# Scale and bias of two norms moved behind the products that read them

## The chip, the cores and the metric

The kernel runs on one core of a Trainium2 chip. A core has five engines with queues of their own: TensorE (PE, with its weight loads as PEld), VectorE (DVE), ScalarE (ACT), GpSimd (POOL) and SyncE (SP), which here issues all DMAs in order. The metric is the device time of one execution in microseconds. Lower is better.

## The reference

One layer of a hybrid diffusion block over 512 latent tokens and 256 context tokens of width 1024, in fp32. What matters for the change, cut down:

```python
# spatial gating, in the token mixer: 8 groups of 128 channels, chunks of 128 tokens
u, v = split(gelu(z_sgu), 2, axis=-1)
v = layer_norm(v, sgu_ln_g, sgu_ln_b)                # over 1024 channels
v = einsum('gpq,bnqgc->bnpgc', sgu_w, v) + sgu_b     # mixes the tokens of a chunk
y_s = u * v

# second sub-layer: norm, modulation, 16 experts that each choose 64 tokens
h = layer_norm(x1) * (1 + sc2) + sh2
aff = softmax(h @ router_w);  gate, idx = top_k(aff.T, 64)
ye = (silu(h[idx] @ exp_w1) * (h[idx] @ exp_w3)) @ exp_w2 * gate
x2 = layer_norm(ALPHA * x1 + gt2 * segment_sum(ye, idx))

# low-rank inputs of the RWKV branch: decay and rate of both directions
w0 + tanh(dw) @ w2          # dw has 64 columns for each direction
a0 + da @ a2
```

`sc2`, `sh2` and their like come from a projection of the conditioning vector (`ada_w`).

## The kernel before, in words

Scratch tiles of 4 KB a partition come from two pools: `T(...)` takes one of 32 slots of the pool `big`, `K(...)` one of 17 of the pool `keep`. A tile's slot goes to a later tile when its last reader is done, and the later tile's first writer waits for that. SyncE, TensorE and ScalarE work in program order all through; VectorE and GpSimd do so inside `manual_schedule()` blocks, and elsewhere a planner orders them by its costs.

Stages in order of time: first norms and modulation; the RWKV columns, eight blocks of 128 channels (L575 on); the gate stage, a list `UNITS` of 32 units with hooks between them (L1035 on); the scan over 12 chunks in both directions by a written plan (`PLAN`, L1062); readout, branch and out projections, the first and second norm and the router; the top-k; and 16 experts, whose weights (`we`, 1 MB a load, a ring of 16 double slots that lies over the pool `big`) are loaded by SyncE as slots come free.

- Token-mixer products split each fp32 operand into a rounded high half H (ScalarE) and the rest L (L160, VectorE or GpSimd), and TensorE adds H·H, H·L and L·H. `zw` streams the weights; `fill` steps it until three split weights wait, so a unit's `fill` makes the weights of the unit two later.
- `pair_x` (L295) takes the columns `dw` and `da` (128 partitions, the two directions in the halves, 256 context then 512 latent tokens). For each direction it makes a tile with the high half in both partition halves (ScalarE copy, DMA to the other half) and one with the rest beside zeros (GpSimd memset, VectorE subtraction): eight tiles in all. `prep_a` multiplies them with `w2` and `a2`.
- In the gate stage's first unit come the spatial norm's statistics and, for each of four tiles `vg`, three VectorE passes (L1031 to L1033): normalise, times `sgu_ln_g`, plus `sgu_ln_b`, the latter two as rows held in all partitions. Then `u_z(g)` projects group g, and `u_s(g)`, two units later, multiplies `vg` with `swt` and adds `sgu_b`.
- The modulation's later rows are summed on VectorE by `ada_part`, one of eight pieces behind each unit's weights. When the eighth is issued, `ada_row` follows in the same unit: two matmuls with `ones` (`adr`), two ScalarE copies, a store to `Mo`.
- `out_ln` makes the second norm `h2` with ScalarE (L146) and then two GpSimd passes over 128x1024 (L1269, L1270) with the rows `sc2` and `sh2`. The router does not read `h2`: it multiplies `x` with router weights that `router_cols` has scaled, out of `R["s2c"]`, which holds `sh2` and 1 + `sc2` by columns.
- `gather` (L1450) multiplies four `h2` tiles with one-hot matrices of two experts' chosen tokens; the result `xe` has channels on partitions and is copied from PSUM by ScalarE, four blocks of 128 channels at a time (one or two for the first pair).

Of the kernel before, what the change touches and what calls it, by code (L numbers as in the profile page):

```python
# [7 lines left out]
F32 = mybir.dt.float32  # L8
# [19 lines left out]
LN_EPS = 1e-5  # L28
GN_EPS = 64e-5
DEC = float(__import__("math").exp(-0.5))  # L30
NKEEP = 17
NBIG = 32

PC = {}
_n = 0
for _k, _w in (("w0", 16), ("a0", 16), ("k_k", 8), ("k_a", 8), ("lnx_g", 8), ("lnx_b", 8), ("r_k", 8),
               ("shift", 81), ("ada_b", 16), ("ln1_g", 8), ("ln1_b", 8)):
    PC[_k] = _n
    _n += _w
NPC = _n  # L40
# [3 lines left out]
def block_kernel(es: ExitStack, tc, x, ctx, cT, ada_w, ada_b, pc, rows, w_ch, w_vs, w2, a2, g2, sgu_w,  # L44
# [247 lines left out]
            V.tensor_tensor(w[h], t[h], w[h].bitcast(F32), OP.subtract)  # L292

    def pair_x(t):
        hs = []  # L295
        for d in range(2):
            h, o = slice(64 * d, 64 * d + 64), slice(64 - 64 * d, 128 - 64 * d)
            x2 = T([128, TT], "xp", F32R)
            S.activation(x2[h], t[h], AF.Copy)
            SY.dma_start(x2[o].bitcast(F32), x2[h].bitcast(F32))  # L300
            lo = T([128, TT], "xl", F32R)
            G.memset(lo[o].bitcast(F32), 0.0)
            V.tensor_tensor(lo[h], t[h], x2[h].bitcast(F32), OP.subtract)
            hs.append((x2, lo))
        return hs

    for k in range(KT):
# [101 lines left out]
    def prep_a(ct, d):  # L409
        s = st_[ct]  # L410
        cs = slice(ct * 128, ct * 128 + 128)
        p2 = P("b2")
        ev = s["ev", d] = []
        for o, lst, src, bias, off in (("g", w2p, dwt, "w0", TC), ("a", a2p, dat, "a0", 0)):
            p = P("b1")
            w, (xh, xl) = lst[d][:, cs], src[d]
            for o_, t_ in ((p, slice(TC, TT)), (p2[:, off:off + TC], slice(0, TC))):
                mm(o_, w, xh[:, t_], True, False)
                mm(o_, w, xl[:, t_], False, True)
            ev.append((o, p, p2[:, off:off + TC], col(bias, d * 8 + ct)))  # L420

    def prep_tanh(ct, d):
# [141 lines left out]
    def ada_part(k, w):  # L564
        wi, k = divmod(k, 8)
        a = late["a", wi]
        V.scalar_tensor_tensor(a, w, sC[:, k:k + 1], a, op0=OP.mult, op1=OP.add)
        if k == 4 and wi < 3:
            ada_begin(wi + 1)
        if k == 7:  # L570
            late["row"].append(a)

    zw.pre = -1
    with tc.manual_schedule():
# [183 lines left out]
    def statics(_):  # L758
        for d in range(2):
            st_tp["zn", d] = K([128, 2, KT, C], "zn")  # L760
            G.memset(st_tp["zn", d], 0.0)
        st_tp["o1"] = K([128, 2, 2, KT, 32], "o1")
        S.activation(st_tp["o1"].rearrange("p a b c i -> p (a b c i)"), zcol.to_broadcast([128, D]), AF.Copy)

    def statics_ro():
# [12 lines left out]
    Md = dp.tile([KT, 128, TL], F32, name="Md")  # L778
    Gd = dp.tile([KT, 128, TL], F32, name="Gd")
    def ada_row(wi):  # L780
        a = late["row"].pop(0)
        m = T([128, D], "mod")
        for h in range(2):
            hs = slice(h * 512, h * 512 + 512)
            p = P("adr")
            mm(p, ones, a[:, hs])
            S.activation(m[:, hs], p, AF.Identity, bias=1.0 if wi == 2 else 0.0)
        spills.append((Mo[wi], m))
# [131 lines left out]
                else:  # L920
                    V.tensor_tensor(dst, dst, p[hs], OP.add)

    sg_g, sg_b, sb_r = row(0), row(1), row(2)
    swt = T([128, 8, 128], "swt")
    SY.dma_start(swt, sgu_w)
    ug, gg_, late_mul = {}, {}, []
    ysH, ysL = [], []
    def u_z(g):
        pl, _ = zmm(zw.get(zi["u", g]), False)
# [3 lines left out]
    def u_s(g):  # L933
        p = P("sgu")
        for i in range(4):
            mm(p[:, i * 128:i * 128 + 128], vg[i][:, g * 128:g * 128 + 128], swt[:, g, :])
        t = T([128, 4, 128], "sgt")
        V.tensor_tensor(t, p.rearrange("p (a b) -> p a b", a=4),
                        sb_r[:, None, g * 128:g * 128 + 128].to_broadcast([128, 4, 128]), OP.add)
        u = ug.pop(g)  # L940
        V.tensor_mul(u, t.rearrange("p a b -> p (a b)"), u)
        if g % 2 == 0:
            ysH.append(K([128, 2, TL], "ysH", F32R))
            ysL.append(K([128, 2, TL], "ysL", F32R))
        H, L = ysH[g // 2][:, g % 2, :], ysL[g // 2][:, g % 2, :]
        S.activation(H, u, AF.Copy)
        V.tensor_tensor(L, u, H.bitcast(F32), OP.subtract)
# [68 lines left out]
    def hook(*key):  # L1016
        for f, a in HOOK.get(key, ()):
            f(a)
# [5 lines left out]
    with tc.manual_schedule():  # L1024
        hook("u", -1)
        mv4 = cp.tile([128, 4, 2], F32, name="mv4")
        for i in range(4):
            ln_stats(vg[i], mv4[:, i, :])
        r4 = rstd(mv4[:, :, 1], 4, LN_EPS)
        for i in range(4):  # L1030
            V.tensor_scalar(vg[i], vg[i], mv4[:, i, 0:1], r4[:, i:i + 1], op0=OP.subtract, op1=OP.mult)  # L1031
            V.tensor_mul(vg[i], vg[i], sg_g)
            V.tensor_add(vg[i], vg[i], sg_b)  # L1033
        lag = []
        for t, j in UNITS:  # L1035
            zw.eng = V
            run[t](j)
            if t == "u":
                lag.append(j)
            if lag and (len(lag) > 2 or t != "u"):  # L1040
                u_s(lag.pop(0))
            if t == "s" and j == 0:
                while lag:
                    u_s(lag.pop(0))
            hook(t, j)
            while len(late_mul) > (t == "b"):
                mul(*late_mul.pop(0))
            if t in "sa":
                flush()
            if late["row"]:  # L1050
                ada_row(late["wi"])
                late["wi"] += 1
        hook("end", 0)

    flush()
# [180 lines left out]
    def out_ln(half, outs, ps):  # L1236
        tiles = [HALF[half][o] for o in outs]
        n = len(tiles)
        mv = sm.tile([128, n, 2], F32, name=nm("mv"), tag=f"mv{n}")
        for q, (o, i) in enumerate(zip(outs, tiles)):  # L1240
            t = acc[i] = K([128, D], "x1")
            st = sm.tile([128, 2, 6], F32, name=nm("st"), tag="st")
            for h, hs in enumerate(HS):
                V.tensor_mul(t[:, hs], ps[o, h], R["gt1"][:, hs])
                V.scalar_tensor_tensor(t[:, hs], R["x", i][:, hs], ALPHA, t[:, hs], op0=OP.mult, op1=OP.add)  # L1245
                V.bn_stats(st[:, h, :], t[:, hs])
            V.bn_aggr(mv[:, q], st)
        yield
        r = rstd(mv[:, :, 1], n, LN_EPS)
        for q, i in enumerate(tiles):  # L1250
            for hs in HS:
                t = acc[i][:, hs]
                V.scalar_tensor_tensor(t, t, mv[:, q, 0:1], R["l1g"][:, hs], op0=OP.subtract, op1=OP.mult)  # L1253
                V.scalar_tensor_tensor(t, t, r[:, q:q + 1], R["l1b"][:, hs], op0=OP.mult, op1=OP.add)  # L1254
        yield
        mv = cp.tile([128, n, 2], F32, name=nm("mw"))
        for q, i in enumerate(tiles):
            ln_stats(acc[i], mv[:, q])
        r = rstd(mv[:, :, 1], n, LN_EPS)
        rk = cp.tile([128, n], F32, name=nm("rk"))  # L1260
        V.tensor_copy(rk, r)
        for q, i in enumerate(tiles):
            ST2[i] = mv[:, q], rk[:, q:q + 1]
        yield
        for q, i in enumerate(tiles):
            t, h = acc[i], K([128, D], "h2")
            h2t[i] = h
            ln_apply(h, t, mv[:, q], rk[:, q:q + 1])
            G.tensor_tensor(h, h, R["sc2"], OP.mult)  # L1269
            G.tensor_tensor(h, h, R["sh2"], OP.add)  # L1270
            yield

    def router_cols():
# [85 lines left out]
    R["rw"] = K([128, KT, NE], "rw")  # L1359
    SY.dma_start(R["rw"], rw)  # L1360
    R["gt1"] = srow(Mo[0], K)
    R["l1g"], R["l1b"] = row(3, K), row(4, K)
    R["sh2"], R["sc2"] = srow(Mo[1], K), srow(Mo[2], K)
    affon = K([NE, 2, TL], "affT")
    affT, on16 = affon[:, 0], affon[:, 1]
    G.memset(on16, 1.0)
# [83 lines left out]
    def gather(e0, k0, k1):  # L1450
        p = P("xe")
        for k in range(k0, k1):
            for i in range(4):
                mm(p[:, (k - k0) * 128:(k - k0) * 128 + 128], h2t[i][:, k * 128:k * 128 + 128], ohs[e0][:, i],
                   start=(i == 0), stop=(i == 3))
        S.activation(xes[e0][:, k0:k1, :], p[:, :(k1 - k0) * 128].rearrange("p (a b) -> p a b", b=128), AF.Copy)

    def route_back(e0):
        oh = ohs.pop(e0)
# [81 lines left out]
    for e in range(NE):  # L1541
# [11 lines left out]
        if e % 2 == 0 and e:  # L1553
            for n in range(2):
                spread(e - 2, HS[n])
            ohT.pop(e - 2), yes.pop(e - 2), gv.pop(e - 2)
    l2 = row(5, K), row(6, K)
    fst = K([128, 4, 4, 6], "fst")
    e, hidT = NE - 1, hidTs.pop(NE - 1)
    c0, cn, prev = 0, 256, None  # L1560
# [37 lines left out]
def _layout(i):  # L1598
# [6 lines left out]
    def blocks(w):  # L1605
# [10 lines left out]
    pc = np.concatenate([  # L1616
        pcols(g["w0"][0]), pcols(g["a0"][0]), pcols(g["k_k"][0]), pcols(g["k_a"][0]), pcols(g["lnx_g"][0]),
        pcols(g["lnx_b"][0]), pcols(g["r_k"][0]), pcols(sw), pcols(ada_b[:2048]),
        pcols(g["ln1_g"][0]), pcols(g["ln1_b"][0])], axis=1)
    return {  # L1620
        "x": g["x"][0],
        "ctx": g["ctx"][0],
# [1 line left out]
        "ada_w": ada_w.reshape(128, 8, 6144),  # L1624
        "ada_b": ada_b[2048:].reshape(8, 512),
        "pc": pc,
        "rows": np.stack([g["sgu_ln_g"][0], g["sgu_ln_b"][0], g["sgu_b"][0].reshape(-1), g["ln1_g"][0],
                          g["ln1_b"][0], g["ln2_g"][0], g["ln2_b"][0]]),
        "w_ch": blocks(w_ch),
        "w_vs": w_vs.reshape(8, 128, 2, 512).transpose(2, 1, 0, 3),  # L1630
        "w2": g["w2"][0],
# [29 lines left out]
```

## Time and profile before

| | |
|---|---|
| median of 3 runs | 2023.44 us (2020.06 to 2025.55) |
| the profiled execution | 2026.06 us, span 2024.3 us |
| TensorE busy in the span | 1768.7 us (87%) |
| VectorE, ScalarE, GpSimd busy | 937.7, 619.8, 234.6 us |
| mean granted TensorE clock | 0.955 of full |
| HBM read, written | 541.78 MB, 47.71 MB |
| expert weights | 376 loads of 1 MB, 32 of 256 KB |

The page cuts the span in 40 slices of 50.6 us. DMA runs at 424 to 427 GB/s from the 23rd slice to the 39th, the experts; before that it moves 109 to 353. VectorE is 6 to 8 tenths busy up to the 21st slice and 1 to 2 tenths after it. The views used below: windows (busy time of each engine in a stretch), the timeline (instructions in order, with the wait in front of each in brackets and who ended it), the groups by line, and the chain of waits that ended last.

### The profile page before, as it was taken

The numbers are of one execution on the slowest core, as the hardware profiler recorded it, in microseconds if no ns is written. First come the engines' busy times: TensorE is split into PE (matmuls) and PEld (weight loads), VectorE is DVE, ScalarE is ACT, GpSimd is POOL, SyncE is SP. The second block draws the span as 40 slices with busy tenths as digits, with TensorE's granted clock in tenths as the row PEclk, the third lists the DMA queues.
The fourth block names the chain that finished last, engine by engine and source line by source line (L and its number), as shares of the span: only waits on it lengthen the run. The fifth ranks groups of instructions, "written<-read, shape, count | busy, mean of one in ns | idle before, by whom it ended". The sixth has DMA issues, their size and how long they took to land.

```text
span 2024.3 us, 32347 instructions
## 1 busy us (share of the span) xinstructions
PE 1768.7 (87%) x13216; PEld 1134.4 (56%) x13216; DVE 937.7 (46%) x1695; ACT 619.8 (31%) x1057; POOL 234.6 (12%) x158
## 2 busy tenths in 40 slices
PE   5989999899988767687978999999998899999895
PEld 3877778778777767686964443434343243434334
DVE  6788885787836667887782111010201101020115
ACT  2777665443246645352331110100111010011101
POOL 4422224000100000044530000000000000000000
PEclk9999999899999888898978999999999999999998
DMA  9355567477785655484458999999999999999995
GB/s 324 115 172 172 177 189 240 145 229 229 247 234 130 143 135 135 109 235 159 142 232 353 426 427 427 426 427 427 427 427 427 426 427 426 427 427 427 427 424 209
DMA packets 364011, 592.41 MB, mean 293 GB/s; under 512 B 220372, under 2 KB 282068, under 8 KB 315736
## 3 DMA queue, kind: packets, MB, share of 16 engines
q1 hardware_dynamic: 363864, 590.35, 79.0%
q8 instruction: 104, 1.70, 0.3%
q14 instruction: 43, 0.35, 0.1%
HBM read 541.78 MB, written 47.71 MB: 291 GB/s over the span
## 4 chain that ended last, share of the span: by engine, by line
DMA 38%; PE 10%; DVE 4%; issue 0%; ACT 0%; DVEq 0%; SPq 0%
DMA we<-in_e 38%; PE hh L74 4%; PE yx L74 1%; PE co L74 1%; PE ye L74 1%; PE xe L74 1%; PE ba L74 1%; PE lg L74 1%; PE hT L1505 0%; DVE x L1245 0%; DVE wk L1423 0%; DVE m L1422 0%; DVE x L1253 0%; DVE x L1254 0%; DVE mt L1187 0%
## 5 line engine op out<-in xcount | busy, mean ns | idle before, releaser
L74 PE MATMUL hh<-we,xe 128*64 128x512 f32 x2048 | 461.4, 595 | 23.6 <-DMA we<-in_e 23.4
L74 PEld LDWEIGHTS hh<-we,xe 128*64 128x64 f32 x2048 | 149.0, 137 | 322.8 <-issue 261.9
L74 PE MATMUL ye<-we,hidT 128*64 128x512 f32 (+1 forms) x1216 | 253.6, 533 | 37.3 <-DMA we<-in_e 36.9
L1495 DVE TENSOR_TENSOR hd<-hd,hh 64x512 f32<-64x512 f32 x64 | 44.1, 690 | 516.6 <-ACT hd L1494 515.6
L74 PE MATMUL zl<-hL,H 128*128 128x512 f32 x816 | 261.1, 401 | 1.1 <-DVE hf L319 1.1
L74 PEld LDWEIGHTS ye<-we,hidT 128*64 128x64 f32 x1216 | 82.4, 136 | 199.7 <-DMA we<-in_e 106.3
L1494 ACT ACTIVATE hd<-hh 64x512 f32<-64x512 f32 x64 | 37.8, 591 | 490.7 <-PE hh L74 490.7
L74 PEld LDWEIGHTS zl<-hL,H 128*128 128x128 f32 x816 | 155.4, 193 | 30.0 <-issue 2.8
L74 PE MATMUL zl<-hL,L 128*128 128x512 f32 x408 | 163.0, 399 | 9.7 <-DVE L L160 9.7
L160 POOL TENSOR_TENSOR L<-w,H 128x1024 fp32r<-128x1024 f32 x54 | 138.2, 2566 | 208.9 <-ACT H L159 155.2
L159 ACT ACTIVATE H<-w 128x1024 fp32r<-128x1024 f32 x91 | 94.8, 1052 | 83.6 <-PE zl L74 25.1
L1588 POOL TENSOR_TENSOR x<-x,row 128x1024 f32<-128x1024 f32 x2 | 4.6, 2340 | 941.1 <-DVE rv L129 941.1
L1513 ACT ACTIVATE ye<-ye 64x512 f32<-64x512 f32 (+1 forms) x34 | 18.8, 554 | 271.6 <-PE ye L74 271.2
L1514 DVE SCALAR_TENSOR_TENSOR ye<-ye,gate,srow 64x512 f32<-64x512 f32 (+1 forms) x38 | 23.8, 663 | 148.4 <-ACT ye L1513 148.1
L74 PEld LDWEIGHTS zl<-hL,L 128*128 128x128 f32 x408 | 78.6, 193 | 21.8 <-DVE L L160 10.8
L710 DVE TENSOR_TENSOR tmpi<-Dt,Xt 128x31 f32<-128x31 f32 (+15 forms) x186 | 63.6, 342 | 19.7 <-DMA Dt<-Asd 14.1
L712 DVE TENSOR_TENSOR Xt<-Xt,tmpi 128x31 f32<-128x31 f32 (+15 forms) x186 | 63.8, 343 | 6.5
L74 PEld LDWEIGHTS xe<-oh,h 128*128 128x128 f32 x512 | 59.6, 196 | 8.9 <-issue 8.9
L74 PE MATMUL co<-ye,ohT 128*128 128x512 f32 (+1 forms) x144 | 64.4, 604 | 0.0
L74 PE MATMUL sc<-al,xx 128*128 128x128 f32 x384 | 49.6, 289 | 16.3 <-DMA xx<-Xkd 7.9
L74 PE MATMUL xe<-oh,h 128*128 128x128 f32 x512 | 61.8, 282 | 0.7 <-DVE oh L1446 0.7
L160 DVE TENSOR_TENSOR L<-w,H 128x1024 fp32r<-128x1024 f32 x37 | 46.7, 1263 | 31.1 <-ACT H L159 23.8
(322 smaller groups left out, 2914.5 us busy)
## 6 DMA issues: line engine op xcount, KB each, us to landing
we<-in_e SPq DMA_DIRECT2D x376, 1024.0 KB, 19.6
w<-in_w_ch SPq DMA_DIRECT2D x51, 512.0 KB, 4.9
w<-in_ada_w SPq DMA_DIRECT2D x32, 512.0 KB, 5.2
xx<-Xkd SPq DMA_DIRECT2D x28, 512.0 KB, 5.5
adaw<-in_ada_w SPq DMA_DIRECT2D x16, 512.0 KB, 10.3
we<-in_e SPq DMA_DIRECT2D x32, 256.0 KB, 5.5
Xkd<-g SPq DMA_DIRECT2D x32, 192.0 KB, 2.7
Ald<-al SPq DMA_DIRECT2D x16, 384.0 KB, 2.3
```

The costliest lines, as they stand in the source:

```text
L74: PE.matmul(o, l, r, start=start, stop=stop, skip_group_check=True)
L159: S.activation(h, t, AF.Copy)
L160: (eng or G).tensor_tensor(l, t, h.bitcast(F32), OP.subtract)
L710: V.tensor_tensor(tv, Dt[:, j, None, j + 1:].to_broadcast([128, m, n]), X[:, 0:m, j:j + 1].to_broadcast([128, m, n]), OP.mult)
L712: V.tensor_tensor(X[:, 0:m, j + 1:], X[:, 0:m, j + 1:], tv, OP.subtract)
L1494: S.activation(hd, pn[n][0:64], AF.Silu)
L1495: V.tensor_tensor(hd, hd, pn[n][64:128], OP.mult)
L1513: S.activation(y, p, AF.Copy)
L1514: V.scalar_tensor_tensor(y, p if same else y, gv[e - j][rs], gt2[rs, cs], op0=OP.mult, op1=OP.mult)
L1588: G.tensor_tensor(acc[i], acc[i], l2[0], OP.mult)
```

## The change

The spatial norm's scale and bias leave the four `vg` tiles. The token product runs on the plainly normalised `vg`; the scale is a column (`sg_g`) in `u_s`, and `sgu_bias` makes the table `sbt` once, the bias column times the sums over `swt`'s tokens, plus `sgu_b`. The second norm's scale and shift leave `h2` and are applied by ScalarE as it copies the gathered block from PSUM, one block of 128 channels at a time. The low-rank inputs lie in six tiles in place of eight. `ada_row` waits until the weight stream is at least four steps past its last piece; the last one comes behind the loop. The pools become 33 and 16 slots, and `o1` moves from `keep` to `big`. The rows `sgu_ln_g`, `sgu_ln_b`, `sh2`, `sc2` are no longer loaded to all partitions.

```diff
-NKEEP = 17
-NBIG = 32
+NKEEP = 16
+NBIG = 33
...
     def pair_x(t):
+        A, B = (T([128, 2, TL], n, F32R) for n in ("xp", "xl"))
+        Cc = T([128, 4, TC], "xc", F32R)
         hs = []
         for d in range(2):
             h, o = slice(64 * d, 64 * d + 64), slice(64 - 64 * d, 128 - 64 * d)
-            x2 = T([128, TT], "xp", F32R)
-            S.activation(x2[h], t[h], AF.Copy)
-            SY.dma_start(x2[o].bitcast(F32), x2[h].bitcast(F32))
-            lo = T([128, TT], "xl", F32R)
-            G.memset(lo[o].bitcast(F32), 0.0)
-            V.tensor_tensor(lo[h], t[h], x2[h].bitcast(F32), OP.subtract)
-            hs.append((x2, lo))
+            for x2, lo, ts in ((A[:, d], B[:, d], slice(TC, TT)), (Cc[:, d], Cc[:, 2 + d], slice(0, TC))):
+                S.activation(x2[h], t[h, ts], AF.Copy)
+                SY.dma_start(x2[o].bitcast(F32), x2[h].bitcast(F32))
+                G.memset(lo[o].bitcast(F32), 0.0)
+                V.tensor_tensor(lo[h], t[h, ts], x2[h].bitcast(F32), OP.subtract)
+            hs.append(((A[:, d], B[:, d]), (Cc[:, d], Cc[:, 2 + d])))
         return hs
...
         if k == 7:
-            late["row"].append(a)
+            late["row"].append((zw.ns, a))
...
-        st_tp["o1"] = K([128, 2, 2, KT, 32], "o1")
+        st_tp["o1"] = T([128, 2, 2, KT, 32], "o1")
...
-    sg_g, sg_b, sb_r = row(0), row(1), row(2)
+    sb_r = row(0)
     swt = T([128, 8, 128], "swt")
     SY.dma_start(swt, sgu_w)
+    sbt = T([128, 8, 128], "sbt")
+
+    def sgu_bias():
+        for h in range(2):
+            p = P("cs")
+            mm(p, ones, swt[:, 4 * h:4 * h + 4, :])
+            for q in range(4):
+                g = 4 * h + q
+                V.scalar_tensor_tensor(sbt[:, g, :], p[:, q * 128:q * 128 + 128], col("sg_b", g),
+                                       sb_r[:, g * 128:g * 128 + 128], op0=OP.mult, op1=OP.add)
...
-        V.tensor_tensor(t, p.rearrange("p (a b) -> p a b", a=4),
-                        sb_r[:, None, g * 128:g * 128 + 128].to_broadcast([128, 4, 128]), OP.add)
+        V.scalar_tensor_tensor(t, p.rearrange("p (a b) -> p a b", a=4), col("sg_g", g),
+                               sbt[:, g, None, :].to_broadcast([128, 4, 128]), op0=OP.mult, op1=OP.add)
...
             V.tensor_scalar(vg[i], vg[i], mv4[:, i, 0:1], r4[:, i:i + 1], op0=OP.subtract, op1=OP.mult)
-            V.tensor_mul(vg[i], vg[i], sg_g)
-            V.tensor_add(vg[i], vg[i], sg_b)
...
                 lag.append(j)
+                if j == 0:
+                    sgu_bias()
...
-            if late["row"]:
+            if late["row"] and late["row"][0][0] < zw.ns - 3:
                 ada_row(late["wi"])
                 late["wi"] += 1
+        if late["row"]:
+            ada_row(late["wi"])
         hook("end", 0)
...
             ln_apply(h, t, mv[:, q], rk[:, q:q + 1])
-            G.tensor_tensor(h, h, R["sc2"], OP.mult)
-            G.tensor_tensor(h, h, R["sh2"], OP.add)
             yield
...
-    R["sh2"], R["sc2"] = srow(Mo[1], K), srow(Mo[2], K)
...
-        S.activation(xes[e0][:, k0:k1, :], p[:, :(k1 - k0) * 128].rearrange("p (a b) -> p a b", b=128), AF.Copy)
+        for k in range(k0, k1):
+            S.activation(xes[e0][:, k, :], p[:, (k - k0) * 128:(k - k0) * 128 + 128], AF.Identity,
+                         scale=R["s2c"][:, 1, k:k + 1], bias=R["s2c"][:, 0, k:k + 1])
```

## Rows read from the trace of the kernel before

**Rows 1.** Windows: busy us of PE, PEld, DVE, ACT, POOL; PEclk, DMA, GB/s

```profile
372.00:387.00 15.00, 6.86 (x20) 5.44 (x20) 12.62 (x11) 1.30 (x2) 0.00 (x0) 0.66 0.21 71
387.00:582.00 195.00, 190.13 (x909) 156.42 (x908) 146.43 (x251) 70.11 (x109) 12.95 (x19) 0.99 0.70 225
960.00:1030.00 70.00, 69.75 (x399) 61.55 (x398) 54.87 (x106) 22.11 (x34) 40.33 (x17) 0.98 0.37 122
1030.00:1073.00 43.00, 19.34 (x101) 16.92 (x99) 33.62 (x116) 13.37 (x24) 9.36 (x4) 0.55 0.82 344
```

**Rows 2.** The same view, the start of the expert weight stream

```profile
1027.00:1046.00 19.00, 14.83 (x84) 13.53 (x82) 15.78 (x56) 3.26 (x6) 2.90 (x2) 0.69 0.95 386
1046.00:1054.00 8.00, 6.16 (x26) 5.23 (x26) 4.54 (x21) 2.17 (x8) 0.00 (x0) 0.50 0.06 14
1075.00:1085.00 10.00, 10.00 (x50) 5.31 (x50) 0.00 (x0) 0.94 (x3) 0.00 (x0) 0.82 0.38 140
1095.00:1985.00 890.00, 829.24 (x3962) 333.66 (x3956) 113.09 (x196) 88.12 (x149) 0.00 (x0) 0.99 1.01 425
```

**Rows 3.** Timeline, TensorE, third u_z: start, us, instruction, wait

```profile
370.71 0.62 PE L74 MATMUL zl<-hL,H 128*128 128x512 f32 x2
...
371.39 0.61 PE L74 MATMUL zl<-hL,H 128*128 128x512 f32 x2
380.14 0.80 PE L74 MATMUL zl<-hL,L 128*128 128x512 f32 x1 [8.14 <-DVE L L160]
...
387.87 1.05 PE L74 MATMUL sgu<-swt,vg 128*128 128x128 f32 x8
```

**Rows 4.** Lines of VectorE, 360 to 390: busy us, mean ns, idle

```profile
L1032 DVE TENSOR_TENSOR vg<-vg,row 128x1024 f32<-128x1024 f32 x4 | 4.9, 1225 | 0.1
L567 DVE SCALAR_TENSOR_TENSOR adacc<-w,sC,adacc 128x1024 f32<-128x1024 f32 x3 | 3.8, 1278 | 0.0
L160 DVE TENSOR_TENSOR L<-w,H 128x1024 fp32r<-128x1024 f32 x3 | 3.7, 1217 | 0.0
```

**Rows 5.** Timeline, TensorE, the first and the third ada_row

```profile
421.40 1.95 PE L74 MATMUL adr<-adacc,ones 128*128 128x512 f32 x4
...
527.78 2.56 PE L74 MATMUL adr<-adacc,ones 128*128 128x512 f32 x4 [3.22 <-DVE adacc L567]
529.35 1.42 PE L74 MATMUL bb<-ysH,H 128*128 128x512 f32 x1
```

**Rows 6.** Lines by form, 0 to 1080: operations of 128x128

```profile
L1154 DVE SCALAR_TENSOR_TENSOR yf<-yT,pcol,bo 128x128 f32<-128x128 f32 x16 | 4.7, 343 | 1.3 <-PE yT L1149 1.3
...
L1156 ACT ACTIVATE yf<-yT,pcol 128x128 f32<-128x128 f32 x16 | 4.5, 365 | 0.0
```

**Rows 7.** Chain of waits that ended last, 1010 to 1075: start, us, what

```profile
1019.37 5.55 DVE x L1245 x2
...
1027.80 2.74 DVE x L1253
...
1032.03 0.66 DVE x L1245
```

**Rows 8.** Timeline, SyncE's queue, start of the scan

```profile
592.21 2.64 SPq L660 DMA_DIRECT2D al<-Ald  x2
```

**Rows 9.** Timeline, ScalarE, start of the scan

```profile
590.42 1.08 ACT L850 ACTIVATE bk<-bk 128x512 f32<-128x512 f32 x2 [4.09 <-DMA Gd<-ga]
```

**Rows 10.** Tile xp: ns min/median/max, first and last start

```profile
L303 DVE TENSOR_TENSOR xl<-dw,xp x2: 950/952/954, 53.2 to 54.2; 64x768 fp32r<-64x768 f32 x2
```

**Rows 11.** Timeline, GpSimd, second norm

```profile
1019.16 2.40 POOL L1269 TENSOR_TENSOR h<-h,srow 128x1024 f32<-128x1024 f32 x1 [3.48 <-ACT h L146]
```

**Rows 12.** Timeline, TensorE, router

```profile
1029.47 1.91 PE L1293 MATMUL h2T<-ident,x 128*128 128x128 f32 x16
1031.22 1.86 PE L74 MATMUL lg<-rw,h2T 128*128 128x16 f32 x16
...
1037.73 6.98 PE L74 MATMUL lg<-rw,h2T 128*128 128x16 f32 x32 [2.10 <-DVE rt L135]
```

More of the change, by code (lines that the diff above doesn't have):

```diff
@@ L36 @@
 for _k, _w in (("w0", 16), ("a0", 16), ("k_k", 8), ("k_a", 8), ("lnx_g", 8), ("lnx_b", 8), ("r_k", 8),
-               ("shift", 81), ("ada_b", 16), ("ln1_g", 8), ("ln1_b", 8)):
+               ("shift", 81), ("ada_b", 16), ("ln1_g", 8), ("ln1_b", 8), ("sg_g", 8), ("sg_b", 8)):
     PC[_k] = _n
@@ L415, in prep_a @@
             p = P("b1")
[L416 to L419, printed above, removed]
+            w = lst[d][:, cs]
+            for o_, (xh, xl) in zip((p, p2[:, off:off + TC]), src[d]):
+                mm(o_, w, xh, True, False)
+                mm(o_, w, xl, False, True)
             ev.append((o, p, p2[:, off:off + TC], col(bias, d * 8 + ct)))
@@ L780, in ada_row @@
     def ada_row(wi):
-        a = late["row"].pop(0)
+        a = late["row"].pop(0)[1]
         m = T([128, D], "mod")
@@ L1361, in block_kernel @@
     R["gt1"] = srow(Mo[0], K)
-    R["l1g"], R["l1b"] = row(3, K), row(4, K)
-    R["sh2"], R["sc2"] = srow(Mo[1], K), srow(Mo[2], K)
+    R["l1g"], R["l1b"] = row(1, K), row(2, K)
     affon = K([NE, 2, TL], "affT")
@@ L1556, in block_kernel @@
             ohT.pop(e - 2), yes.pop(e - 2), gv.pop(e - 2)
-    l2 = row(5, K), row(6, K)
+    l2 = row(3, K), row(4, K)
     fst = K([128, 4, 4, 6], "fst")
@@ L1618, in _layout @@
         pcols(g["lnx_b"][0]), pcols(g["r_k"][0]), pcols(sw), pcols(ada_b[:2048]),
-        pcols(g["ln1_g"][0]), pcols(g["ln1_b"][0])], axis=1)
+        pcols(g["ln1_g"][0]), pcols(g["ln1_b"][0]), pcols(g["sgu_ln_g"][0]), pcols(g["sgu_ln_b"][0])], axis=1)
     return {
@@ L1626, in _layout @@
         "pc": pc,
-        "rows": np.stack([g["sgu_ln_g"][0], g["sgu_ln_b"][0], g["sgu_b"][0].reshape(-1), g["ln1_g"][0],
-                          g["ln1_b"][0], g["ln2_g"][0], g["ln2_b"][0]]),
+        "rows": np.stack([g["sgu_b"][0].reshape(-1), g["ln1_g"][0], g["ln1_b"][0], g["ln2_g"][0], g["ln2_b"][0]]),
         "w_ch": blocks(w_ch),
```

## The prediction

> **What bounds the kernel now.** I read the page's forty slices first, then the windows by stage, then the waits of the engine that is fullest in each. The windows show three kinds of stage. The gate stage (387 to 582 us) and the readout stage (960 to 1030) belong to TensorE: 190.1 of 195.0 us and 69.75 of 70.0 busy [rows 1]. Two short stretches belong to VectorE: 372 to 387, where TensorE works 6.9 of 15 us at a mean granted clock of 0.66 while VectorE is 12.6 busy, and 1030 to 1073, the router and the top-k, where TensorE works 19 of 43 us at 0.55 [rows 1]. From 1095 on the expert weights set the pace: DMA share 1.01 at 425 GB/s [rows 2]. So the questions are who ends last in the two VectorE stretches, and whether time saved ahead of the experts reaches the weight stream.
>
> **1. The gate stage's start.** The third `u_z` has its first two matmuls at 371.39, and the next one starts at 380.14, 8.14 us late: it waits for the low half L of its weights, which VectorE splits (L160) [rows 3]. VectorE has that split in its queue behind the normalisation of four `vg` tiles. The change takes eight passes out of that queue, four of L1032 and four of L1033, 1.225 us each by their group (L1033 has the same count and mean): 9.8 us [rows 4]. The split that ended at 380.1 then ends near 370.4. It is wanted at 372.0, so the whole wait goes. With it goes the slow stretch behind it: 22 matmuls were left and the next work (sgu) starts at 387.87, so they took 7.73 us; at the pace before the wait (three in 0.68 us, from the starts 370.71 and 371.39) they take 5.0. That is 2.7 us more [rows 3].
>
> What comes in: two matmuls of `ones` against `swt` between the first and the second `u_z`. The same shape in `ada_row` (four records) lasts 1.95 us with its drain [rows 5]; between 1.2 (an estimate without the drain) and 1.95 I take 1.5. Eight VectorE operations of 128x128 from PSUM cost 0.343 us each by L1154 [rows 6], 2.7 us. They stand behind the split that was late and ahead of the next `ada_part` and split (1.28 and 1.22 us [rows 4]), which then end near 375.6. The fourth `u_z` wants that split near 378.5. This cover is 3 us; what exceeds it comes back as a wait of TensorE. `u_s` swaps an addition for a scalar_tensor_tensor of the same shape, 0.66 us by the undisturbed L1245 [rows 7], eight times, where VectorE is not late. Part 1: 8.1 + 2.7 - 1.5 = 9.3 us saved.
>
> **2. `ada_row` two units later.** Its matmuls stand in TensorE's queue right behind the unit whose `fill` issues the eighth `ada_part`. For the third row TensorE waits 3.22 us for it; then its matmuls take 2.56 us against 1.95 for the first row, and the matmul behind them 1.42, where two of that shape at full pace last 0.61 [rows 3, 5], so one some 0.4. Moved behind two more units, the input is ready: 3.2 + 0.6 + 1.0, 4.8 us. The moved step also issues two ScalarE copies and a store of `Mo` each time, all later by two units; nothing reads `Mo` before the readout.
>
> The fourth row is another matter. It moves from the seventh `a` unit to behind the eighth, so its copies follow the last gate copy on ScalarE, and its store stands on SP behind the six loads of `prep_load(5)` (two of them take 2.64 us to issue [rows 8], six some 8). Scratch slots are short here: ScalarE's first `bk` copy of the scan waits 4.09 us for a gate store to give one back [rows 9], and all of ScalarE's scan work queues behind it. `o1` now takes a scratch slot too, and the pool is larger by one. So the start of the scan lies between 4 us better (the larger pool ends that wait) and 8 us worse (a copy waits for the late store). The count of slots is level, and the late store is the one thing that is clearly worse: I take 1 us worse, near the row as it stands. Part 2: 3.8 us saved.
>
> **3. `pair_x` in six buffers.** Four 64x768 copies, DMAs, memsets and subtractions become eight smaller ones of each. The subtraction takes 0.953 us [rows 10]; by the short forms' fixed parts (0.343 for 128 columns [rows 6]) splitting one costs at most 0.3 us, 1.2 us in all on VectorE, as much on ScalarE. No engine waits for their result: what TensorE waits for in that stage are the `vs` evictions. The two slots that this frees, and the third from `NBIG`, meet no wait of TensorE there. Bounds: 2 us either way; taken 0, since no wait names these tiles.
>
> **4. The second norm without its GpSimd passes.** Eight passes go, each about 2.4 us. The first of four that run back to back starts at 1019.16 [rows 11], and just there the chain of waits carries two L1245 at 5.55 us together and an L1253 at 2.74, where an undisturbed L1245 takes 0.66 [rows 7]. That is 4.2 + 2.1 us at these two places. The gain is more than that, since it is the third tile's norm that is late. TensorE ends its out projection at 1029.47 and transposes two tiles, and runs the first 16 router products in 1.86 us; then it waits for the third tile, and the next 32, from 1037.73, take 6.98 us, a low clock's pace [rows 12]; the last tile's transposes and products follow in that queue. With VectorE 6 us earlier, only the last tile's own chain behind 1029.5 is left: residual, statistics, rstd and affine, some 7 us by undisturbed lengths, with the router products at full clock under it. I put the top-k 8 to 11 us earlier; 6 if only the two blocked places come back, 2 if the planner orders VectorE's small operations worse. I take 10. The other four passes lie beside the top-k, which the chain passes without them: nothing to gain.
>
> Does the weight stream follow? It starts at 1027, as scratch slots come free, and then loses twice: 1046 to 1054 moves 14 GB/s (a slot held by a transposed tile of the router), 1075 to 1085 moves 140 (ring full, TensorE just starting) [rows 2]. At 425 that is 7.7 + 6.7 us of stream not used. A router that is 10 us earlier is paid out of these 14, so nearly all of it reaches the end; I leave 0.5 for new hold-ups: 9.5 us. The gather's 19 evictions become 64 of one 128-column block each, 0.365 us by L1156, which also scales by a column [rows 6]: 45 more are at most 16 us of ScalarE time spread under 890 us of weight stream; where TensorE leads, in the first expert, 0.1 us once. Without that cover it would be those 16 us. The rows `sc2` and `sh2` are no longer loaded ahead of the branch weights (2 x 512 KB, 2.5 us at 425): 0 to 2.5 us, taken 0.9, since VectorE bounds most of what follows.
>
> **Sum.** 9.3 + 3.8 + 0 + 9.5 + 0.9 = 23.5 us. The profiled execution took 2026.06 us (span 2024.3 and 1.8 around it), so 2002.5 for it; it stood 2.6 above the median of the runs, 2023.44, so 1999.9 for a median.
>
> **Rivals.** (a) The stream does not follow the router. The slot of the first or second weight tile may, in a pool that is moved by one slot, lie under a tile that the router holds to its end. For it: the 8 us hole at 1046 is such a hold-up. Against: 386 GB/s from 1027 on, ahead of it [rows 2]. The router's 10 us are then worth 0 to 4, the sum is 14 to 18: 2008 us.
>
> The Trainium skill, page "SBUF — State Buffer", section "A bandwidth-pool intuition that's wrong (but worth ruling out)", says that HBM is almost always the end-to-end bottleneck and gives about 358 GB/s for a core. The expert stream shows 425 GB/s [rows 2], so on the rate the measurement decides. As a rule it speaks for (a): engine time ahead of a stream is worth nothing unless the stream starts earlier.
>
> (b) VectorE's passes are not what ends last at 372, since the split needs its high half and its weights too. Against: the split's group shows no idle time in front of it [rows 4]. Part 1 is then 1.5 us lost, the sum 12.7: 2011. (c) Slower: the kept pool of 16 tiles is one short in the experts. Nine stay through it (four `acc`, four `h2`, `gt2`), and a pair of experts uses seven or eight more. If a tile of each pair waited for a back product of the expert before (some 14 us), TensorE would lose 14 a pair, against a slack of 61 us in 890 [rows 2], 8 for each of seven and a half pairs: 7 x 6 = 42 us against 23.5 saved: 2042. It decides from 11.5 us of wait a pair. Against it: counted through a pair, the eighth tile is asked for only after the hidden product has given one back.
>
> **Chances.** Forecast 0.67 (own range 1990 to 2006), (a) 0.18, (b) 0.07, (c) 0.04, and 0.04 for a loss at the scan's start that eats most of the gain. About 0.3% (6 us) is what a measurement of this kernel can tell from no change. Faster takes in the forecast, (a) and most of (b), 0.90; within 0.3% 0.05; slower 0.05, (c) and a little. The range for 8 in 10 reaches from all bounds good to (a) and (b): 1989 to 2013.
>
> **What would show it.** Right: no wait of TensorE for L160 near 372 and a granted clock of 1.0 there; `adr` matmuls without a wait; L1245 near 0.7 us everywhere; the gather's start some 23 us earlier. Wrong: a new wait of ScalarE at the first `bk` copies, more than 14 us of holes in the stream before its full rate, or waits of TensorE for `xe` in the experts.

## The result and the profile after

| | before | after |
|---|---|---|
| median | 2021.75 us (4 runs, 2018.74 to 2025.55) | 2035.04 us (4 runs, 2033.93 to 2036.65) |
| profiled execution | 2026.06 us | 2034.86 us |
| ratio, after to before | | 1.0065, 95% interval 1.0045 to 1.0086 |

The changed kernel is slower by 13 us; forecast was 23.5 us faster. The windows of the changed kernel by stage (columns: stretch, its length, busy time and count of PE, PEld, DVE, ACT, POOL, then granted clock, DMA share and GB/s), answering to [rows 1, 2]:

```profile
372.00:387.00 15.00, 15.00 (x88) 13.17 (x87) 11.22 (x19) 6.12 (x12) 0.95 (x1) 1.00 0.29 113
...
1030.00:1073.00 43.00, 22.13 (x125) 17.35 (x123) 26.91 (x95) 13.44 (x25) 0.00 (x0) 0.60 0.77 314
1095.00:1985.00 890.00, 819.42 (x3850) 332.91 (x3848) 112.47 (x194) 99.62 (x190) 0.00 (x0) 0.99 1.01 420
```

Two things turned out as forecast. TensorE is busy for all of the 15 us from 372, at full clock (6.9 at 0.66 before). And GpSimd has nothing left beside the router. But the experts run at 420 GB/s with the DMA share at 1.01, where the kernel before had 425 at the same share [rows 2]. A full queue that moves less is not a wait: each byte costs more. The profiled executions add up so (starts of the first gather product and of the last combine product, from the tile views): gather 1073.1 before, 1065.2 after, 7.9 us gained and not 23; from there to the last combine product 929.7 before, 946.3 after, 16.6 lost; the rest 0.1. That is +8.8, the difference of these two executions; the medians differ by 13.

The first `sgu` products of TensorE, answering to [rows 3] (start, duration, engine, line, operation; a wait would stand in brackets at the end):

```profile
382.14 1.05 PE L74 MATMUL sgu<-swt,vg 128*128 128x128 f32 x8
```

They start at 382.14 where they started at 387.87, with no wait before them. That is 5.7 us earlier and not 9.3, since the stage ahead of the gate ends later: its last `zv` product starts at 363.8 and not at 360.3. The third deferred row, answering to [rows 5], has lost its wait of 3.22 us; its four matmuls take 1.88 us where they took 2.56, and the two behind them 1.03 where one took 1.42:

```profile
525.39 1.88 PE L74 MATMUL adr<-adacc,ones 128*128 128x512 f32 x4
526.70 1.03 PE L74 MATMUL zl<-hL,H 128*128 128x512 f32 x2
```

On VectorE the second norm is no longer held up [rows 7]: two L1245 (now L1259) take 1.28 us at the place where they took 5.55, and L1253 (now L1267) 0.74 where it took 2.74.

```profile
1018.48 1.28 DVE L1259 SCALAR_TENSOR_TENSOR x<-srow,x 128x512 f32<-128x512 f32 x2
...
1022.03 0.74 DVE L1267 SCALAR_TENSOR_TENSOR x<-x,mv,row 128x512 f32<-128x512 f32 x1
```

What is new stands at the scan's start. First ScalarE, then SyncE's queue:

```profile
584.63 2.20 ACT L851 ACTIVATE bk<-bk 128x512 f32<-128x512 f32 x4 [1.97 <-DMA Gd<-ga]
586.85 1.57 ACT L802 ACTIVATE o<-l 32x256 f32<-32x256 f32 x4
594.51 3.15 ACT L686 ACTIVATE ap<-sc 64x256 f32<-64x256 f32 x8 [6.09 <-DMA Mo<-mod]
```

```profile
582.07 0.91 SPq L379 DMA_DIRECT2D Gd<-ga  x2
583.07 1.31 SPq L661 DMA_DIRECT2D al<-Ald  x2
584.47 0.68 SPq L662 DMA_DIRECT2D xx<-Xkd  x1
585.27 1.25 SPq L661 DMA_DIRECT2D al<-Ald  x2
586.94 0.84 SPq L662 DMA_DIRECT2D xx<-Xkd  x1
587.87 1.78 SPq L379 DMA_DIRECT2D Mo<-mod  x1
```

ScalarE's first eviction of the next attention block (L686) waits 6.09 us for the store `Mo<-mod`. That store was issued at 587.87, behind the six loads of `prep_load(5)`; the tile `ap` waits for it as the next owner of the row's scratch slot (as allocated, the two tiles have the same address; e4 below tests what the wait costs). In the kernel before the same store went out at 588.36, ahead of those loads. TensorE's first `up` product then starts at 599.75, where it started at 599.67 before: of the gate's gain nothing is left here.

And transfers are dearer, in the expert stream and in the scan. The expert stream from 1150 to 1950, before and then after (packets, bytes, rate; then count, size and median us from issue to landing):

```profile
DMA packets 46842, 341.37 MB, mean 427 GB/s; under 512 B 5200, under 2 KB 5200, under 8 KB 5200
...
we<-in_e SPq DMA_DIRECT2D x325, 1024.0 KB, 19.6
```

```profile
DMA packets 46210, 336.75 MB, mean 421 GB/s; under 512 B 5132, under 2 KB 5132, under 8 KB 5132
...
we<-in_e SPq DMA_DIRECT2D x320, 1024.0 KB, 19.8
```

The scan's loads, 640 to 820, before and then after, same shapes and sizes:

```profile
al<-Ald SPq DMA_DIRECT2D x24, 128.0 KB, 4.0
uv<-Vd SPq DMA_DIRECT2D x21, 128.0 KB, 3.8
ro<-Rhd SPq DMA_DIRECT2D x16, 128.0 KB, 4.3
```

```profile
al<-Ald SPq DMA_DIRECT2D x24, 128.0 KB, 5.0
uv<-Vd SPq DMA_DIRECT2D x20, 128.0 KB, 5.0
ro<-Rhd SPq DMA_DIRECT2D x16, 128.0 KB, 5.6
```

The scan's loads `xx` and `sv` go the same way (5.6 to 6.3 us, 3.2 to 4.4). Its loads `tp` and `x` (2.6 to 2.7, 2.6 to 2.3) and its store `Xsd` (4.1 to 4.0) do not.

One edit touches all of these buffers at once, and the prediction did not price it: the table of columns (`pcol`) gets 16 more columns for `sg_g` and `sg_b`, 64 bytes a partition. The diff ahead of the prediction leaves this line out:

```diff
-               ("shift", 81), ("ada_b", 16), ("ln1_g", 8), ("ln1_b", 8)):
+               ("shift", 81), ("ada_b", 16), ("ln1_g", 8), ("ln1_b", 8), ("sg_g", 8), ("sg_b", 8)):
```

The table is the second tile of the constants, so every tile behind it moves: as allocated, the expert weight buffers begin at 97280 = 380 x 256 before and at 93248 = 364 x 256 + 64 after (one `keep` slot of 4096 bytes fewer, 64 bytes more).

### The profile page after: what moved, and what is told of

It reads as the page before. It is cut to its first block, busy times and chain, and to the rows that moved or that the text cites. A ratio compares the mean times of both kernels' runs of the same rounds, so it can differ in the third digit from the quotient of the medians.

```text
span 2033.1 us, 32436 instructions
## 1 busy us (share of the span) xinstructions
PE 1777.3 (87%) x13220; PEld 1143.8 (56%) x13220; DVE 930.9 (46%) x1699; ACT 633.0 (31%) x1106; POOL 212.8 (10%) x154
## 4 chain that ended last, share of the span: by engine, by line
DMA 43%; PE 13%; DVE 9%; issue 1%; ACT 1%; SPq 1%; POOL 0%; DVEq 0%; POOLq 0%; ACTq 0%
DMA we<-in_e 40%; PE hh L74 4%; DVE tmpi L711 2%; DVE Xt L713 2%; PE yx L74 2%; DMA xx<-Xkd 1%; PE ye L74 1%; PE xe L74 1%; PE l L74 1%; PE qs L74 1%; PE yp L74 1%; PE zp L74 1%; PE bk L850 1%; PE up L74 1%; DMA Dt<-Asd 1%
## 5 line engine op out<-in xcount | busy, mean ns | idle before, releaser
L74 PE MATMUL hh<-we,xe 128*64 128x512 f32 x2048 | 468.2, 599 | 29.5 <-DMA we<-in_e 29.5
L74 PEld LDWEIGHTS hh<-we,xe 128*64 128x64 f32 x2048 | 156.1, 138 | 327.6 <-issue 261.7
L160 POOL TENSOR_TENSOR L<-w,H 128x1024 fp32r<-128x1024 f32 x54 | 137.8, 2558 | 243.7 <-ACT H L159 197.6
L711 DVE TENSOR_TENSOR tmpi<-Dt,Xt 128x31 f32<-128x31 f32 (+15 forms) x186 | 63.6, 342 | 16.5 <-DMA Dt<-Asd 10.9
L74 PEld LDWEIGHTS zc<-hC,H 128*128 128x128 f32 x288 | 54.0, 188 | 12.7 <-POOL hC L322 0.4
```

The source lines that it names most:

```text
L74: PE.matmul(o, l, r, start=start, stop=stop, skip_group_check=True)
L160: (eng or G).tensor_tensor(l, t, h.bitcast(F32), OP.subtract)
L711: V.tensor_tensor(tv, Dt[:, j, None, j + 1:].to_broadcast([128, m, n]), X[:, 0:m, j:j + 1].to_broadcast([128, m, n]), OP.mult)
```

## The experiments

Each was measured beside runs of the kernel before, and its ratio is against those. Their medians lie between 2020.7 and 2024.4 us, so differences between the medians of two rows are rough by some us; the ratio is also not the plain quotient of two medians. "Experts" is the time from the first gather product to the last combine product in the profiled execution.

| run | buffers past a multiple of 256 B | stream GB/s | gather at | experts | median us | ratio (95%) |
|---|---|---|---|---|---|---|
| before | 0 | 427 | 1073.1 | 929.7 | | |
| after | 64 | 421 | 1065.2 | 946.3 | 2035.0 | 1.0065 (1.0045 to 1.0086) |
| e1 | 0 | 427 | 1053.7 | 931.6 | 2009.5 | 0.9933 (0.9916 to 0.9950) |
| e2 | 64 | 421 | 1077.6 | 943.1 | 2044.5 | 1.0095 (1.0075 to 1.0115) |
| e3 | 0 (256 more) | 427 | 1071.6 | 929.0 | 2022.9 | 0.9995 (0.9980 to 1.0010) |
| e6 | 128 | 421 | 1073.9 | 943.2 | 2041.7 | 1.0096 (1.0079 to 1.0113) |
| e9 | 32 | 420 | 1084.2 | 945.4 | 2053.5 | 1.0146 (1.0125 to 1.0167) |
| e5 | 64, weights 0 | 427 | 1072.9 | 932.0 | 2020.3 | 0.9980 (0.9961 to 0.9999) |
| e7 | 0 | 427 | 1062.2 | 930.2 | 2017.8 | 0.9961 (0.9946 to 0.9976) |
| e8 | 0 | 427 | 1065.1 | 928.8 | 2015.3 | 0.9955 (0.9933 to 0.9976) |
| e4 | 0 | 426 | 1047.6 | 931.9 | 2003.7 | 0.9900 (0.9879 to 0.9920) |
| e10 | 0 | 426 | 1048.2 | 929.9 | 2002.0 | 0.9891 (0.9866 to 0.9915) |
| e12 | 0 | 427 | 1051.9 | 931.1 | 2006.6 | 0.9917 (0.9899 to 0.9934) |
| e11 | 0 | 427 | 1051.5 | 929.7 | 2005.1 | 0.9910 (0.9888 to 0.9932) |

**e1 to e3: do the 64 bytes do it?** e1 is the changed kernel, e2 and e3 the kernel before, each with fill behind the table and nothing else:

```diff
-    pcol = cp.tile([128, NPC], F32, name="pcol")
-    SY.dma_start(pcol, pc)
+    pcol = cp.tile([128, NPC + 112], F32, name="pcol")   # e1; +16 in e2, +64 in e3
+    SY.dma_start(pcol[:, :NPC], pc)
```

> The changed kernel with 448 unused bytes per partition behind the column table, so that every tile behind the table (keep and big pools, weight buffers) begins at a multiple of 512 B again, as in the kernel before (weight buffers from 93696 = 183 x 512 instead of 93248 = 182 x 512 + 64). Nothing else differs. Theory A (the 64 bytes that the change adds to the table shift the buffers and every transfer into or out of them gets dearer): the weight stream goes from 420 to 426 GB/s, uv and ro of the scan from 5.0 and 5.6 us to 3.8 and 4.3, xx from 6.3 to 5.6, and the kernel is faster than the one before: 1995 to 2012 us. Rival B (the stream is slower because of something else, the place of the inputs in HBM after the rows and the table changed size, or the pools' new numbers): stream stays at 420 GB/s and the time at 2035 us.

> The kernel before with 64 unused bytes per partition behind the column table and nothing else: the inputs in HBM, the pools' counts and the program stay, the buffers move by 64 B (weight buffers from 97344 = 190 x 512 + 64). Theory A: the stream falls from 427 to 420 GB/s (some 13 us of the 941 us of experts), the scan's transfers uv and ro go to 5.0 and 5.6 us, and the kernel loses 20 to 35 us: 2042 to 2057 us. Rival B (place in HBM, or pools' counts): 2022 us, 427 GB/s.

> The kernel before with 256 unused bytes per partition behind the column table and nothing else (weight buffers from 97536 = 190 x 512 + 256). If theory A is right and what matters is a boundary of 512 B, this one loses as much as the shift by 64 B; if a boundary of 256 B or less does, it stays at 2022 us and 427 GB/s. Rival B: 2022 us.

e1 and e2 came out as theory A said, from both sides: 448 bytes of fill make the changed kernel 25.6 us faster by medians, 64 bytes of fill make the kernel before 20 us slower, with the program, the inputs in HBM and the pools as they were. The stream of e1, and then stream and scan loads of e2:

```profile
DMA packets 46851, 341.37 MB, mean 427 GB/s; under 512 B 5202, under 2 KB 5202, under 8 KB 5216
```

```profile
DMA packets 46207, 336.75 MB, mean 421 GB/s; under 512 B 5129, under 2 KB 5129, under 8 KB 5129
```

```profile
uv<-Vd SPq DMA_DIRECT2D x24, 128.0 KB, 4.8
al<-Ald SPq DMA_DIRECT2D x24, 128.0 KB, 4.7
ro<-Rhd SPq DMA_DIRECT2D x16, 128.0 KB, 5.4
```

e3 answers its own question: 512 B are not needed, a shift by 256 B costs nothing. Its stream:

```profile
DMA packets 46841, 341.37 MB, mean 427 GB/s; under 512 B 5200, under 2 KB 5200, under 8 KB 5200
```

It is the transfers that get dearer and not the engines' work on the shifted tiles: between 590 and 1020 us ScalarE's `bk` evictions take 601 ns in the mean before and in e2, its `ap` evictions 378 and 378, VectorE's `al` products 422 and 421.

**e6 and e9: which boundary?** The same edit with 32 and with 8 columns of fill.

> The kernel before with 128 unused bytes per partition behind the column table (weight buffers from 97408 = 190 x 512 + 128). A shift by 64 B cost 1.4% of the stream's rate (427 to 421 GB/s), one by 256 B nothing. Theory A (the boundary that counts is 128 B: a packet of 8 KB then touches 65 stretches instead of 64, 1.6% more, and one of 256 B three instead of two): no loss, 427 GB/s, 2022 us. Rival B (the boundary is 256 B, 33 stretches for 32): the stream stays at 421 GB/s or falls to 414, 2042 us or more.

> The kernel before with 32 unused bytes per partition (weight buffers from 97312 = 190 x 512 + 32). Theory A (only whether a packet begins at the boundary counts): the same loss as with 64 B, 421 GB/s and 2042 us. Rival B (pieces of 64 B are what counts beside the boundary): a greater loss, under 415 GB/s and over 2050 us. Rival C: 32 B costs nothing, 2022 us.

Their streams, e6 and then e9:

```profile
DMA packets 46239, 336.95 MB, mean 421 GB/s; under 512 B 5137, under 2 KB 5137, under 8 KB 5137
```

```profile
DMA packets 46046, 335.61 MB, mean 420 GB/s; under 512 B 5108, under 2 KB 5108, under 8 KB 5108
```

128 B cost as much as 64 in the stream and, within the intervals, in the kernel: theory A of e6 (a boundary of 128 B) falls, the boundary is 256 B. With 32 B the rate falls to 420 and not below 415, so e9's rival B falls on the rate, though its time (over 2050 us) came out; the kernel is 9 to 12 us slower than with 64 or 128, against e9's theory A. The gather is 7 to 10 us later than in e2 and e6, so most of it lies ahead of the experts. There the packets themselves show the order. The queue's line for the scan, 640 to 820 (packets, MB, the time that the packets took as a share of 16 engines), for the kernel before, e2, e6 and e9:

```profile
q1 hardware_dynamic: 90267, 24.92, 60.6%
q1 hardware_dynamic: 89983, 25.04, 69.1%
q1 hardware_dynamic: 90143, 24.96, 63.6%
q1 hardware_dynamic: 87720, 24.47, 69.8%
```

For each MB that is 13% more packet time with 64 B, 5% with 128 and 17% with 32, where the saturated stream lost 1.4 to 1.7%. In these executions the gather comes 4.5, 0.8 and 11.1 us later than in the kernel before: the dearer the packets, the later.

**e5: how much of it is the stream?** The fill stands only in front of the weight buffers:

```diff
+    fill = es.enter_context(tc.tile_pool(name="fill", bufs=1))
+    fill.tile([128, 112], F32, name="fill")
     wpool = es.enter_context(tc.tile_pool(name="wide", bufs=1, reuse_waits="tile"))
```

> The changed kernel with 448 bytes of fill only in front of the expert weight buffers: these begin at a multiple of 512 B (93696), every tile of the stages ahead of them stays 64 B off it. Theory A (a shift by 64 B makes each transfer dearer by itself): the stages up to the gather go as in the changed kernel (gather at 1065), the stream runs at 426 GB/s, which over some 400 MB is 13 us: 2021 to 2023 us; the remaining 12 us of the 25.5 that the full fill gave back are the stages ahead. Rival B (the stream alone carries all of it): 2010 us. Rival C (the shift hurts only through small transfers of the early stages): 2035 us.

```profile
DMA packets 46829, 341.32 MB, mean 427 GB/s; under 512 B 5195, under 2 KB 5195, under 8 KB 5195
```

This is theory A: the stream is back at 427 GB/s while the gather stays late (in this execution, the slowest of twelve, later still than the changed kernel's 1065.2). By medians the 25.6 us divide into 14.8 for the stream (2035.0 to 2020.3) and 10.8 for the stages ahead (2020.3 to 2009.5); by the ratios into some 17 and 9.5. The first number is also what the experts' time gives (946.3 against 931.6 of e1). The second is looser: e5's runs spread from 2004.9 to 2028.3.

**e7 and e8: the two main parts alone**, on the kernel before with all buffers at multiples of 256 B. e7 has the change's edits of the bias row, `sbt`, `sgu_bias`, `u_s` and the two `vg` passes, and the two new columns with fill; e8 those of the two GpSimd passes, the rows `sc2` and `sh2` and `gather`.

> The kernel before with the gate's part alone (scale and bias of the spatial norm behind the token product, their columns in the table, the bias tiles), and 448 bytes of fill so that all buffers begin at multiples of 512 B; the deferral of the rows, the pair buffers, the pools and the second norm as before. Theory A (the step as forecast): 9.3 us less, 2015 us, the scan starting 9 us earlier and ending as much earlier. Rival B: the scan's own waits on transfers take part of it back: first keys 8 us earlier, end of scan 3 to 5 us earlier, 2019 to 2021 us.

> The kernel before with the second norm's part alone: no GpSimd passes, no rows sc2 and sh2, scale and shift in the gather's 64 evictions; the column table, all pools and the gate as before, so all buffers stay where they were. Theory A (the step as forecast): gather about 9 to 11 us earlier and the whole of it at the end, 2014 us. Rival B (the stream does not follow the router): gather earlier, the stream's end unmoved but for 3 us, 2021 us.

The window of e7 in which TensorE had stood, and VectorE's norm in e8:

```profile
372.00:387.00 15.00, 15.00 (x88) 13.17 (x87) 11.15 (x17) 6.76 (x13) 0.95 (x1) 1.00 0.10 19
```

```profile
1017.38 1.28 DVE L1245 SCALAR_TENSOR_TENSOR x<-srow,x 128x512 f32<-128x512 f32 x2
...
1020.93 0.74 DVE L1253 SCALAR_TENSOR_TENSOR x<-x,mv,row 128x512 f32<-128x512 f32 x1
```

e7: 7.9 us faster by its ratio (4.9 to 10.9), 5.3 by the medians, between its theory A and its rival B. In its profiled execution the first `sgu` product stands 9.5 us earlier, the first keys (`bk`) 9.0, the last `yp` product 8.8 and the gather 10.9: what was gained at the gate stayed, as theory A said. e8: 9.1 us (4.9 to 13.6), 7.8 by the medians, theory A. The gather is 8.0 us earlier, of which 6.0 lie behind the last `yx` product, and the last combine product 8.9: the stream followed. The 2.0 us ahead of that `yx` product are not shown to come from the change: e3, with the program of before, has 1.5 there.

**e4: the store of the fourth row.** On e1, one line more:

```diff
         if late["row"]:
             ada_row(late["wi"])
+        flush()
         hook("end", 0)
```

> The changed kernel with the 448 bytes of fill (2009.5 us), and one line more: the store of the fourth deferred row is issued before the loads of unit 5 (a flush ahead of the end hook) and not behind them. In the aligned run the first keys of the scan stand 11.0 us earlier than in the kernel before, but the first up products only 3.0 us: ScalarE's first eviction of the next unit's attention (L686) waits 6.52 us for the store Mo<-mod, issued at 584.33, since its scratch slot is that of the row. Theory A: the store is issued about 4.5 us earlier, the wait shrinks to about 2 us, and 3 to 5 us of it reach the end: 2004.5 to 2006.5 us. Rival B: the loads behind the store become late instead, or the later waits of the scan absorb it: 2009 us.

ScalarE in e1 and then in e4, and SyncE in e4:

```profile
583.36 1.57 ACT L802 ACTIVATE o<-l 32x256 f32<-32x256 f32 x4
591.46 3.15 ACT L686 ACTIVATE ap<-sc 64x256 f32<-64x256 f32 x8 [6.52 <-DMA Mo<-mod]
```

```profile
581.58 2.06 ACT L851 ACTIVATE bk<-bk 128x512 f32<-128x512 f32 x4 [3.23 <-DMA Gd<-ga]
583.67 1.58 ACT L802 ACTIVATE o<-l 32x256 f32<-32x256 f32 x4
585.27 3.16 ACT L686 ACTIVATE ap<-sc 64x256 f32<-64x256 f32 x8
```

```profile
579.02 0.91 SPq L379 DMA_DIRECT2D Gd<-ga  x2
580.02 0.41 SPq L379 DMA_DIRECT2D Mo<-mod  x1
580.52 1.88 SPq L661 DMA_DIRECT2D al<-Ald  x2
```

The store goes out 4.3 us earlier and the wait is gone whole, more than theory A had. The first `up` product comes 6.2 us earlier, the gather 6.1, the last combine product 5.8: what that wait cost came through to the end unchanged. By the medians it is 5.8 us too.

**e10: the deferral itself.** On e1, `ada_row` at once again:

```diff
-            if late["row"] and late["row"][0][0] < zw.ns - 3:
+            if late["row"]:
                 ada_row(late["wi"])
                 late["wi"] += 1
-        if late["row"]:
-            ada_row(late["wi"])
```

> The changed kernel with the 448 bytes of fill (2009.5 us) and the deferred rows of adaLN taken up as soon as they are there, as in the kernel before; the fourth row's scratch buffer and the rest as in the changed kernel. It shows what the deferral by two units is worth. Theory A (as forecast: the third row's wait of 3.22 us and its low clock come back, 4.8 us; the fourth row's store then stands earlier and the 6.52 us wait of ScalarE goes): the two nearly cancel, 2007 to 2010 us, with the wait of TensorE for the third row at 520 to 530 in the trace again and no wait for Mo<-mod at the scan's start. Rival B (the wait for the row is hidden): 2003 to 2005 us. Rival C (the store stays behind the loads): 2013 to 2015 us.

TensorE at the third row, then SyncE at the scan's start:

```profile
520.60 2.94 PE L74 MATMUL adr<-adacc,ones 128*128 128x512 f32 x4 [2.42 <-DVE adacc L568]
```

```profile
581.29 0.38 SPq L379 DMA_DIRECT2D Mo<-mod  x1
...
582.26 1.90 SPq L661 DMA_DIRECT2D al<-Ald  x2
```

The wait for the row is back (2.42 us), the store of the fourth row stands ahead of the loads, and the kernel is 7.5 us faster than e1 by medians. Against e4, which has the deferral and the early store, there is no difference (0.9891 and 0.9900; the intervals leave room for some 5 us). The traces show what the scan absorbs: e4 is 3.2 us ahead of e10 at the first keys (571.6 against 574.8), 2.1 at the first `up` product, 0.6 at the last `yp` product and 0.6 at the gather. So the deferral is worth nothing that can be measured at the end, and its store cost 6 us: nearest to rival B of e10, 1 us below its range. With e4 level it is the fastest of all kernels here.

**e12 and e11: what is left.** e12 adds to e4 a flush ahead of the hooks of every `a` unit; e11 gives e4 the pools of before (17 and 32) with `o1` kept.

> The kernel of the last set with fill and the fourth row's store ahead of unit 5's loads (2003.7 us), and a flush of the stored ga tiles before the hook of every a unit, so that Gd of unit 6 is stored before the loads of the scan's first values are queued. ScalarE's first key eviction still waits 3.23 us for Gd<-ga. Theory A (that wait is for the store of unit 6): it goes, 2001 us. Rival B (it is for the store of unit 7, which stays where it is, behind loads of x and tp at 579): no change, 2003 to 2005 us.

> The kernel with fill and the fourth row's store ahead of unit 5's loads (2003.7 us), with the pools of the kernel before (17 kept, 32 scratch buffers; weight buffers from 97792 = 191 x 512) and the scan's tile o1 in the kept pool again; the pair buffers stay packed in six. Theory A (as forecast, the pools and the pair buffers are worth nothing either way): 2001 to 2006 us. Rival B (o1's place in the scratch pool costs at the scan's start, where ScalarE clears it 2.3 us after it could): the up products start 2 us or more earlier and the kernel is at 2000 us or below. Rival C (one scratch buffer fewer makes loads of the scan or of the router late): 2008 us or more.

ScalarE's first key evictions in e12:

```profile
576.18 1.09 ACT L851 ACTIVATE bk<-bk 128x512 f32<-128x512 f32 x2 [0.35 <-PE l L74]
581.20 1.09 ACT L851 ACTIVATE bk<-bk 128x512 f32<-128x512 f32 x2 [3.94 <-DMA Gd<-ga]
```

Two of the four now go early, and the other two wait 3.94 us for the store of unit 7, which went out at 578.86: rival B, and no gain (2006.6 us). e11 is level with e4 (theory A): the pools and `o1`'s place are worth nothing that reaches the end. At the gate's start they show: the last `zv` product ahead of it starts at 359.4 in e11 and at 360.9 to 363.0 in e1, e4, e10 and e12, which have the new pools; at the first keys (572.5 in e11, 571.6 in e4) nothing of it is left.

## Why the prediction was wrong

**The failing step is the sum.** "9.3 + 3.8 + 0 + 9.5 + 0.9 = 23.5 us" has no term for the column table. Of the sixteen columns it priced the operations that read them and not the 64 bytes by which they move every later buffer. That term is 25.6 us (e1 against the changed kernel; e2 has 20 on the other kernel), larger than the whole forecast. The 425 GB/s of [rows 2] were taken as given for the changed kernel; this rate moved, and with it the scan's loads. The chances then left 0.05 for slower, from mechanisms of waiting alone. The first two signs for "Right" (no wait for L160 at full clock, `adr` without a wait) came out in a kernel that was slower: no sign named the rate.

**Part 1** was right: the wait went, the clock stayed at 1.0, TensorE stays busy through the stretch with the eight bias operations in it. Forecast 9.3; alone 9.5 at the first `sgu` product of e7 and 7.9 (4.9 to 10.9) at the end.

**Part 2** was wrong in sign. The mechanism was named ("its store stands on SP behind the six loads of `prep_load(5)`") with 8 us as its worst end, and then "I take 1 us worse", by the row as it stood before. It took 6, one group later than the prediction's sign for "Wrong" looked: the wait at the first `bk` copies shrank (1.97 us for 4.09), and `ap` waited. And the 4.8 us of the third row did not reach the end: e10, with that wait, is as fast as e4, without it. For part 2 the forecast was 3.8 us saved; the runs show some 6 lost.

**Part 3**: the 0 fits what was measured. e11 tests the pools and `o1`; the packing itself was not run alone, but e11, which has it, starts its first `sgu` product no later than e7, which has not (377.7 and 378.4).

**Part 4** was right in sum: forecast 10.4, alone 9.1 (4.9 to 13.6). The size inside was not: behind the last `yx` product e8 gained 6.0 us where "I take 10", which is the lower end ("6 if only the two blocked places come back"). The rest of the 9.1 is not shown to be the change's, so that the sum fits is in part luck. That the stream follows held: in e1 the gather is 19.4 us earlier than before and the last combine product 17.5. So rival (a) fell, and (b) with e7. Rival (c) fell too: the aligned experts, with 16 kept tiles, take 931.6 us against 929.7.

Without the shift and with the store in front (e4), the change does 20 us (16 to 24) of the 23.5 forecast.

## What to carry to other kernels

A tile that grows moves every tile allocated behind it: after any edit to constants, look at the offset of the DMA-fed buffers against a multiple of 256 B, and in the trace at the rate of a saturated stretch, which must not change when the program does not. A step that is deferred takes its stores along: find what stands in front of them in the queue, and who gets the slot that they hold. Where a bound is wide because a slot's next owner is unknown, look the owner up in the allocation: here the far end was 8 us with a chance of 0.04, and 6 came.

## What the runs showed of the hardware

Loads into buffers that begin 32, 64 or 128 B past a multiple of 256 B ran at 420, 421 and 421 GB/s in a saturated stream of 8 KB packets, and at 427 at multiples of 256 B. The scan's loads in rows of 256 B lose more: the median of `ro` (128 KB) was 5.0 to 5.6 us in the five traces with shifted scan buffers (after, e2, e5, e6, e9) and 3.5 to 4.6 in the nine without, that of `uv` 4.2 to 5.0 and 3.5 to 3.8. The loads `tp` and `x` (64 KB each) and the store `Xsd` landed no later in e2 than before (2.6 and 2.5 us against 2.6 and 2.6, 4.1 against 4.1).

The Trainium skill, page "DMA: Bandwidth & Descriptors", section "How a descriptor splits into AXI transactions", says that a descriptor is cut into transactions of 256 B that must start at multiples of 256 B, so that one beginning elsewhere is cut from the boundary below it. The page words this for reads; what moved here is the destination in SBUF. The boundary agrees with e3, e6 and e9. The size does not follow from its counts: by that rule an 8 KB packet would be 33 transactions for 32, 3.1% more, or 257, 258 and 260 beats of 32 B for 256 with the three shifts, 0.4 to 1.6% more (estimates from the page's rule, on the SBUF side); the runs have 1.4 to 1.7% with all three. The order of the beats, most with 128 B, is also the reverse of the scan's packets, where 32 B cost the most (17%) and 128 B the least (5%). Why that is so stays open.
